# A pooling stage with four bands built and four copied, its scale on the bands, its residual bias on DVE and its order held by the source

## The chip, the cores and the metric

The kernel runs on one core of a Trainium2 chip. The time is the device time of one execution in microseconds, the median of several runs. The core's engines are TensorE (PE in the profile, its weight loads PEld), VectorE (DVE), ScalarE (ACT), GpSimd (POOL) and SyncE (SP), which issues every DMA here. Each engine works through its own queue in order, and semaphores hold one engine back until another has finished what it needs.

## The reference

A trunk of two layers over 512 tokens of 1024 channels, float32 throughout. Layer 0 mixes tokens by causal pooling, layer 1 by windowed attention; each is followed by a gated MLP with a short causal convolution. Only the pooling of layer 0 and the first matmuls of its MLP matter here:

```python
def pool_mixer(h, w, b, scale):          # h: RMS-normed tokens
    csum = jnp.cumsum(hf, axis=1)
    for gi, win in enumerate((2, 4, 8, 16)):      # 256 channels each
        mean = (c - lo) / jnp.minimum(t1, win)    # mean of the last win tokens
        outs.append(mean - hf[..., sl])
    p = jnp.stack(outs, axis=2)
    y = jnp.einsum('bsgc,gcd->bsgd', p, w) + b
    return y.reshape(B, S, D) * scale

h = h + pool_mixer(rms_norm(h, norm_mix[0]), ...)
h = h + conv_glu_ffn(rms_norm(h, norm_ffn[0]), ...)
```

## The kernel before

Channels lie on partitions: the residual h is eight tiles h 0 to h 7 of 128 channels by 512 tokens. Every product of weights and activations is made of three matmuls, since both sides are split into a rounded half (`_h`) and the rest (`_l`): `mm3` (L82) issues h times h at L84, h times l at L85, l times h at L86. ScalarE makes the rounded half, and DVE or POOL subtracts it to get the rest.

The pooling stage (`pool_mixer`, L256) goes like this. POOL first builds eight bands of 128 by 144 (L162 to L172): four for the inner tiles, one for each window, and four for the edge at the first token, where the window is cut and the divisor comes from `rc` (L160). Twelve warm-up products (L263) run on PE meanwhile. For each of four tiles of 128 tokens (L264), ScalarE sums the squares (L266), ScalarE and DVE turn the sum into 1/rms (`rsqrt_mean`, L177), DVE scales the 1024 columns of the token tile by it (L268), and PE multiplies each of the eight channel blocks with its band (L271); a float32 product takes two passes of PE, so a tile has 16. The eight results lie in the eight PSUM banks. Then `split_scaled` (L247) gives px_h on ScalarE (L251) and px_l on DVE (L252) for each bank, with a weight tile of the MLP split behind every second one, its rest on POOL (L99). Last, for each block c: ScalarE adds the bias to h c (L299), PE makes the pooled product (six matmuls), DVE adds it to h c with the scale (L305), `split_scaled` gives f0x_h and f0x_l, and `norm.add` squares h c on ScalarE (L215) and adds it up on POOL (L224). The products use six banks in turn, 0 to 5 and then 0 and 1.

The MLP follows (`mlp_in`): its first group is four products at once in the banks 2 to 5, each over k = 0 to 7, with f0x of block k as the moving side; then the statistics of the norm (L230). A first matmul on a bank waits until the previous content has been read: by L305 of blocks 2 to 5 in this case.

All loads go through SP's queue in the order of the source: four token tiles, two pooling weight tiles, the vectors, three MLP weight tiles, then h 0 to h 7 (L290), and then the weights of the MLP as buffers come free.

The order of each engine's instructions is made by a planner: among the instructions whose inputs its own model of time takes to be ready, the first of the source goes first. So the order on an engine can differ from the source. `tc.keep_in_program_order(ins)` puts `ins` behind the instruction traced just before it on the same engine; nothing in the kernel before uses it.

Of the kernel before, what the change touches and what calls it, by code (L numbers as in the profile page):

```python
# [31 lines left out]
WINDOWS = (2, 4, 8, 16)  # L32
BW = P + 16
# [6 lines left out]
EPS = 1e-6  # L40
# [17 lines left out]
def trunk(ctx: ExitStack, tc: tile.TileContext, x_tok, x_t, vecs, w_pool, w_kq, w_v, w_o, w_in, w_out, out_a, out_b):  # L58
    nc = tc.nc
    V, A, G, T = nc.vector, nc.scalar, nc.gpsimd, nc.tensor  # L60
# [8 lines left out]
    def small(pool, n, words, dt=F32, **kw):  # L69
        return pool.tile([P, words], dt, **kw)[:, :n]  # L70
# [17 lines left out]
    def fetch(src, n, name):  # L88
        raw = wp.tile([P, 1024], F32, tag="raw", name=f"{name}_raw", bufs=3)
        nc.sync.dma_start(raw[:, :n], src)  # L90
        return raw

    def weights(src, n, name, eng=None, raw=None):

        raw = raw or fetch(src, n, name)
        h = wp.tile([P, 1024], F32R, tag="wh", name=f"{name}_h")
        l = wp.tile([P, 1024], F32R, tag="wl", name=f"{name}_l")
        A.activation(h[:, :n], raw[:, :n], AF.Copy)  # L98
        (eng or V).tensor_tensor(l[:, :n], raw[:, :n], h[:, :n].bitcast(F32), ALU.subtract)  # L99
        return h, l  # L100

    def part(w, k, m=P):
        return tuple(t[:, k * m : (k + 1) * m] for t in w)

    def in_weights(layer, j, s, eng=None, raw=None):
        return weights(w_in[layer, j, s], D, f"wi{layer}_{j}_{s}", eng, raw)

    def out_weights(layer, half, m):
        w = [
# [5 lines left out]
    def kept_weights(layer, half, m):  # L115
# [41 lines left out]

    rc = small(fst, 16, 64, name="rc")
    for t in range(15):
        G.memset(rc[:, t : t + 1], 1.0 / (t + 1))  # L160
    band = fst.tile([P, 8, BW], F32, name="band")
    for edge in (True, False):  # L162
        for g, w in enumerate(WINDOWS):
            b = band[:, 4 * edge + g, :]
            G.memset(b, 1.0 / w)
            G.affine_select(b, b, [[1, BW]], ALU.is_ge, 0.0, base=0, channel_multiplier=-1)
            G.affine_select(b, b, [[-1, BW]], ALU.is_ge, 0.0, base=w - 1, channel_multiplier=1)
            G.affine_select(b, b, [[1, BW]], ALU.not_equal, 1.0 / w - 1.0, base=0, channel_multiplier=-1)
            if edge:
                f = b[:, : w - 1]  # L170
                G.affine_select(f, rc[:, : w - 1], [[1, w - 1]], ALU.is_ge, 0.0, base=0, channel_multiplier=-1)
                G.tensor_tensor(f, f, ident[:, : w - 1], ALU.subtract)  # L172
# [4 lines left out]
    def rsqrt_mean(dst, ssq, n, root=False):  # L177


        def tmp(k, dt=F32):  # L180
            return small(sm, n, 16, dt, tag=f"rs_{k}", name=f"rs_{k}", bufs=4)

        v = tmp("v")
        y = tmp("y")
        if root:
            A.activation(y, ssq, AF.Sqrt, bias=eps, scale=1.0 / D)
            V.tensor_scalar(v, ssq, -0.5 / D, -0.5 * EPS, ALU.mult, ALU.add)
            V.reciprocal(y, y)
        else:
            V.tensor_scalar(v, ssq, 1.0 / D, EPS, ALU.mult, ALU.add)  # L190
            sh = tmp("i", I32)
            V.tensor_scalar(sh, v.bitcast(I32), 1, None, ALU.logical_shift_right)
            V.tensor_scalar(y.bitcast(I32), sh, -1.0, float(0x5F3759DF), ALU.mult, ALU.add)
            V.tensor_scalar(v, v, -0.5, None, ALU.mult)
        t = tmp("t")
        steps = 1 if root else 3
        for it in range(steps):
            z = dst if it == steps - 1 else y
            if n == 1:
                V.scalar_tensor_tensor(t, y, y, v, ALU.mult, ALU.mult)  # L200
# [43 lines left out]
            A.activation(rb[:, lo:hi], ps[:, lo:hi], AF.Copy)  # L244
            return rb

    def split_scaled(src, g, name):  # L247

        xh = xp.tile([P, S], F32R, tag="xh", name=f"{name}_h")
        xl = xp.tile([P, S], F32R, tag="xl", name=f"{name}_l")  # L250
        A.activation(xh, src, AF.Copy, scale=g)  # L251
        V.scalar_tensor_tensor(xl, src, g, xh.bitcast(F32), ALU.mult, ALU.subtract)  # L252
        return xh, xl


    def pool_mixer(norm, xs, ws):  # L256
        r0 = small(fst, NT, 32, name="r0")
        ss0 = small(fst, NT, 32, name="ss0")

        warm = small(fst, BW, 192, name="warm")  # L260
        V.memset(warm, 0.0)
        for i in range(12):
            T.matmul(banks[-1][:, :BW], lhsT=warm[:, :P], rhs=warm, start=True, stop=True)  # L263
        for i in range(NT):  # L264
            junk = fst.tile([P, D], F32, tag="junk", name=f"junk{i}")
            A.activation(junk, xt[:, i, :], AF.Square, accum_out=ss0[:, i : i + 1])  # L266
            rsqrt_mean(r0[:, i : i + 1], ss0[:, i : i + 1], 1, root=True)
            V.tensor_scalar(xt[:, i, :], xt[:, i, :], r0[:, i : i + 1], None, ALU.mult)  # L268
            n = min(BW, S - i * P)
            for c in range(NC):  # L270
                T.matmul(  # L271
                    banks[c][:, i * P : i * P + n],
                    lhsT=xt[:, i, c * P : (c + 1) * P],
                    rhs=band[:, (0 if i else 4) + c // 2, :n],
                    start=(i == 0),
                    stop=(i == NT - 1),
                    skip_group_check=True,
                )
        wpool = []
# [11 lines left out]
        pool_x = []
        for c in range(NC):
            pool_x.append(split_scaled(banks[c], col(V_NM + c), f"px{c}"))
            if c % 2:
                ws.append(in_weights(0, *pre[c // 2], G, raws[c // 2]))
# [87 lines left out]
    with tc.tile_pool(name="ap", bufs=2) as ap:  # L383
# [88 lines left out]
        for j in range(NT):  # L472
            ps = vps[j // 2][:, (j % 2) * 256 : (j % 2 + 1) * 256]
# [157 lines left out]
    with tc.tile_pool(name="fp1", bufs=2) as fp:  # L631
# [33 lines left out]
        w = {m: (kept_weights if m == NB else out_weights)(1, 1, m) for m in range(NB, NC)}  # L665
# [5 lines left out]
        for m in range(NB, NC):  # L671
# [15 lines left out]
        ps = bank("aux")  # L687
        for x, t in enumerate((norm3.acc, sq)):
            for j in range(2):
# [3 lines left out]
                    rhs=ones[:, :2],  # L693
# [78 lines left out]
```

## Time and profile before

| | us |
|---|---|
| median of 3 runs (932.06 to 932.5) | 932.32 |
| the profiled execution, its own time | 932.39 |
| its span, first to last instruction | 930.6 |
| PE busy, share of the span | 915.2, 98% |
| DVE busy | 574.8, 62% |
| ACT busy | 427.3, 46% |
| POOL busy | 135.1, 15% |

The busy times are of the whole span. The pooling stage is the first 28 us of it and the first group of the MLP ends at 51 us, so the shares say little about the stage: there one reads the instructions in order of time, with their start, how long they took, and in brackets how long the engine had been idle before and who released it. The ends of matmuls are modelled in the profile; their starts, and the distance from one start to the next, are what counts for PE. A line that stands for several instructions in a row has their number behind an x.

### The profile page before, as it was taken

The page shows a single profiled execution, that of the slowest core. Times are in us where ns is not written, and L with a number is a line of the kernel's source. Part 1 is how long each engine was busy: PE and PEld are TensorE (multiplying, and loading weights), DVE is VectorE, ACT ScalarE, POOL GpSimd, SP SyncE. Part 2 cuts the span into 40 slices and gives each one's busy share as a digit, 9 for nine tenths or more (in the row PEclk, how much of TensorE's full clock was granted, in tenths as well). Part 3 has the DMA queues.
Part 4 walks back from the last instruction along what each step waited for, and adds up shares of the span by engine and source line. Part 5 has one row for each costly group of instructions (what it writes and reads, how often), then busy time and mean ns, then how long its engine had stood idle before and what let it go on. Part 6 is the DMA issues. An engine that isn't in the chain of part 4 may idle for free.

```text
span 930.6 us, 11682 instructions
## 1 busy us (share of the span) xinstructions
PE 915.2 (98%) x4419; PEld 771.5 (83%) x4419; DVE 574.8 (62%) x945; ACT 427.3 (46%) x690; POOL 135.1 (15%) x217
## 2 busy tenths in 40 slices
PE   8999999999999999999899999999999999999996
PEld 7788888888888888898788888888888888888896
DVE  5679766335777754456777482987743377777433
ACT  7655443223444443337787451644422244444532
POOL 9600000000000001325654140000000000000022
PEclk9999999999999999999999999999999999999999
DMA  9133222333223223322111041242233422322312
GB/s 333 67 113 113 93 84 80 93 128 113 91 91 105 65 87 106 114 91 68 50 43 46 2 158 39 98 139 104 63 93 100 136 91 91 111 80 63 95 60 91
DMA packets 28855, 88.13 MB, mean 95 GB/s; under 512 B 3200, under 2 KB 4352, under 8 KB 28800
## 3 DMA queue, kind: packets, MB, share of 16 engines
q1 hardware_dynamic: 28800, 87.40, 28.5%
q8 instruction: 34, 0.56, 0.2%
q14 instruction: 21, 0.17, 0.1%
HBM read 85.29 MB, written 2.10 MB: 94 GB/s over the span
## 4 chain that ended last, share of the span: by engine, by line
PE 92%; ACT 3%; DVE 2%; POOL 2%; issue 1%; POOLq 0%; ACTq 0%
PE bank L84 30%; PE bank L85 30%; PE bank L86 30%; PE bank L548 1%; PE bank L578 1%; ACT sc L565 1%; DVE q L464 1%; ACT px_h L251 0%; POOL sc L570 0%; PE bank L241 0%; ACT q_u L457 0%; DVE sc L551 0%; ACT wi_h L98 0%; PE bank L271 0%; ACT th L581 0%
## 5 line engine op out<-in xcount | busy, mean ns | idle before, releaser
L224 POOL TENSOR_TENSOR n_acc<-n_acc,n_sq 128x512 f32<-128x512 f32 (+1 forms) x28 | 39.1, 1395 | 716.4 <-ACT n_sq L215 709.8
L98 ACT ACTIVATE wi_h<-wi_raw 128x1024 fp32r<-128x1024 f32 x88 | 93.0, 1061 | 109.0 <-PE bank L85 100.5
L85 PE MATMUL bank<-f0x_l,wi_h 128*128 128x512 f32 x352 | 137.1, 389 | 0.8 <-DVE f0x_l L252 0.8
L84 PE MATMUL bank<-f0x_h,wi_h 128*128 128x512 f32 x352 | 137.3, 390 | 0.0
L84 PE MATMUL bank<-f1x_h,wi_h 128*128 128x512 f32 x352 | 137.2, 390 | 0.0
L84 PE MATMUL bank<-zh,wo_h 128*128 128x512 f32 (+1 forms) x363 | 137.1, 378 | 0.0
L86 PE MATMUL bank<-f0x_h,wi_l 128*128 128x512 f32 x352 | 137.0, 389 | 0.0
L86 PE MATMUL bank<-f1x_h,wi_l 128*128 128x512 f32 x352 | 137.0, 389 | 0.0
L85 PE MATMUL bank<-f1x_l,wi_h 128*128 128x512 f32 x352 | 137.0, 389 | 0.0
L86 PE MATMUL bank<-zh,wo_l 128*128 128x512 f32 (+1 forms) x363 | 136.6, 376 | 0.0
L85 PE MATMUL bank<-zl,wo_h 128*128 128x512 f32 (+1 forms) x363 | 136.6, 376 | 0.0
L99 DVE TENSOR_TENSOR wi_l<-wi_raw,wi_h 128x1024 fp32r<-128x1024 f32 x84 | 102.6, 1223 | 49.2 <-ACT wi_h L98 37.3
L98 ACT ACTIVATE wo_h<-wo_raw 128x768 fp32r<-128x768 f32 (+1 forms) x70 | 57.5, 823 | 120.2 <-PE bank L85 108.5
L313 DVE TENSOR_TENSOR c_u<-bank,n_rb 128x512 f32<-128x512 f32 x88 | 59.9, 687 | 75.9 <-PE bank L86 75.9
L99 DVE TENSOR_TENSOR wo_l<-wo_raw,wo_h 128x768 fp32r<-128x768 f32 (+1 forms) x66 | 60.3, 914 | 54.4 <-ACT wo_h L98 54.2
L86 PEld LDWEIGHTS bank<-zh,wo_l 128*128 128x128 f32 x363 | 68.3, 188 | 12.5
L84 PEld LDWEIGHTS bank<-zh,wo_h 128*128 128x128 f32 x363 | 68.3, 188 | 12.3
L85 PEld LDWEIGHTS bank<-zl,wo_h 128*128 128x128 f32 x363 | 68.3, 188 | 12.3
L85 PEld LDWEIGHTS bank<-f0x_l,wi_h 128*128 128x128 f32 x352 | 66.1, 188 | 14.6 <-DVE f0x_l L252 1.2
L84 PEld LDWEIGHTS bank<-f0x_h,wi_h 128*128 128x128 f32 x352 | 66.1, 188 | 14.2 <-DVE h L305 0.4
L86 PEld LDWEIGHTS bank<-f1x_h,wi_l 128*128 128x128 f32 x352 | 66.1, 188 | 13.9
L316 ACT ACTIVATE c_t<-c_u,vec 128x512 f32<-128x512 f32 x88 | 70.6, 811 | 15.3 <-DVE c_u L313 14.5
(173 smaller groups left out, 1488.7 us busy)
## 6 DMA issues: line engine op xcount, KB each, us to landing
wi_raw<-w_in SPq DMA_DIRECT2D x88, 512.0 KB, 3.2
wo_raw<-w_out SPq DMA_DIRECT2D x31, 384.0 KB, 3.0
wo_raw<-w_out SPq DMA_DIRECT2D x31, 320.0 KB, 2.8
kq_raw<-w_kq SPq DMA_DIRECT2D x10, 512.0 KB, 3.2
wo_raw<-w_o SPq DMA_DIRECT2D x8, 512.0 KB, 3.2
xt<-x_tok SPq DMA_DIRECT2D x4, 512.0 KB, 5.2
h<-x_t SPq DMA_DIRECT2D x8, 256.0 KB, 7.5
wpool_raw<-w_pool SPq DMA_DIRECT2D x2, 512.0 KB, 8.5
```

What stands on the lines that cost most here:

```text
L84: T.matmul(ps, lhsT=wh, rhs=xh, start=start, stop=False, **kw)
L85: T.matmul(ps, lhsT=wh, rhs=xl, start=False, stop=False, **kw)
L86: T.matmul(ps, lhsT=wl, rhs=xh, start=False, stop=stop, **kw)
L98: A.activation(h[:, :n], raw[:, :n], AF.Copy)
L99: (eng or V).tensor_tensor(l[:, :n], raw[:, :n], h[:, :n].bitcast(F32), ALU.subtract)
L224: eng.tensor_tensor(self.acc[:, lo:hi], self.acc[:, lo:hi], sq[:, lo:hi], ALU.add)
L313: V.tensor_tensor(u, ps, rb, ALU.mult)
L316: A.activation(t, u, AF.Identity, bias=col(V_CB + layer * 2 * NF + m), scale=cw[2])
L464: V.tensor_tensor(t[dst], u[src], t[src].bitcast(F32), ALU.subtract)
L548: T.matmul(o, lhsT=qt, rhs=kt[:, kk : kk + 256], start=x == 0, stop=x == 1)
L565: A.activation(t, t, AF.Exp, bias=neg[:, i : i + 1], scale=-1.0, accum_out=den[:, i : i + 1])
L578: T.transpose(ps[:, i * P : (i + 1) * P], sc[i // 2][:, i % 2, kb * P : (kb + 1) * P], ident)
```

## The change

Eight parts, all in the pooling stage and in the helpers that it calls:

- POOL builds four bands instead of eight, and the small edge parts apart; the rest of the edge bands is copied by DVE (`edge_copy`), two before the tile loop and two inside the first tile. The memsets of `rc` and of the bands go from POOL to DVE.
- The 1/rms of a token tile scales the four bands (`sband`, 4 x 144 columns) instead of the token tile (1024 columns).
- In the first tile DVE squares and sums half of the columns, ScalarE the other half.
- The rest of the first pooling weight is taken on DVE instead of POOL.
- The rest of an MLP weight tile that POOL makes ahead is made in four instructions of 256 columns instead of one of 1024.
- The bias of h c is added on DVE (`bias`) instead of ScalarE.
- The fourth MLP weight tile is fetched and split behind the last pooled product (step "w").
- `pin` holds the order on DVE and ScalarE. The string `order` gives it: m is the split of a bank (with the MLP weight behind every second one), p the pooled product, b the bias, t the total into h c, n the split of the new h c and its square.

```diff
+    def weights(src, n, name, eng=None, raw=None, step=1024, pin=lambda ins: ins):
...
+        pin(A.activation(h[:, :n], raw[:, :n], AF.Copy))
+        for a in range(0, n, step):
+            o = slice(a, min(a + step, n))
+            (eng or V).tensor_tensor(l[:, o], raw[:, o], h[:, o].bitcast(F32), ALU.subtract)
...
+        return weights(w_in[layer, j, s], D, f"wi{layer}_{j}_{s}", eng, raw, 256 if eng else 1024, pin)
...
+    pin = tc.keep_in_program_order
...
-        G.memset(rc[:, t : t + 1], 1.0 / (t + 1))
+        V.memset(rc[:, t : t + 1], 1.0 / (t + 1))
...
+    def edge_copy(g):
+        a = WINDOWS[g] - 1
+        pin(V.tensor_copy(band[:, 4 + g, a:], band[:, g, a:]))
+    for g, w in enumerate(WINDOWS):
+        b = band[:, g, :]
+        V.memset(b, 1.0 / w)
...
+        f = band[:, 4 + g, : w - 1]
+        G.affine_select(f, rc[:, : w - 1], [[1, w - 1]], ALU.is_ge, 0.0, base=0, channel_multiplier=-1)
+        G.tensor_tensor(f, f, ident[:, : w - 1], ALU.subtract)
+        if g < 2:
+            edge_copy(g)
...
-            V.tensor_scalar(xt[:, i, :], xt[:, i, :], r0[:, i : i + 1], None, ALU.mult)
+            sband = fst.tile([P, 4, BW], F32, tag="sband", name=f"sband{i}", bufs=2)
+            e = 0 if i else 4
+            pin(V.tensor_scalar(sband[:, :, :n], band[:, e : e + 4, :n], r0[:, i : i + 1], None, ALU.mult))
...
-                    rhs=band[:, (0 if i else 4) + c // 2, :n],
+                    rhs=sband[:, c // 2, :n],
...
-            A.activation(h[c], h[c], AF.Identity, bias=bs[:, c : c + 1])
+        def bias(c):
+            pin(V.tensor_scalar(h[c], h[c], bs[:, c : c + 1], None, ALU.add))
+
+        def total(c):
+            pin(V.scalar_tensor_tensor(h[c], ps[c], col(V_PS + c), h[c], ALU.mult, ALU.add))
+
+        def normed(c):
+            xs.append(split_scaled(h[c], col(V_NFF + c), f"f0x{c}", pin))
             norm.add(c)
+        order = "m0 m1 p0 p1 b0 b1 m2 m3 p2 p3 m4 m5 t0 t1 b2 b3 p4 p5 m6 m7 t2 t3 p6 p7 w n0 b4 b5 t4 t5 n1 b6 b7 t6 t7 n2 n3 n4 n5 n6 n7"
+        for step in order.split():
+            if step == "w":
+                ws.append(in_weights(0, *pre[3], G))
...
```

## Rows read from the trace of the kernel before

**Rows 1.** The page, part 1: busy time, share and instructions of each engine.
```profile
PE 915.2 (98%) x4419; PEld 771.5 (83%) x4419; DVE 574.8 (62%) x945; ACT 427.3 (46%) x690; POOL 135.1 (15%) x217
```
**Rows 2.** Waits of PE, whole span: us in total, times, longest us.
```profile
PE bank L85 <- DVE f0x_l L252: 0.8, 1, 0.8
```
**Rows 3.** PE by time, 0 to 52 us: start us, us, what, times, idle before.
```profile
1.17 5.09 PE L263 MATMUL bank<-warm 128*128 128x144 f32 x24 [1.17 <-DVE warm L261]
7.89 0.36 PE L271 MATMUL bank<-band,xt 128*128 128x144 f32 x1 [1.64 <-DVE rs_y L188]
12.52 4.50 PE L271 MATMUL bank<-band,xt 128*128 128x144 f32 x36 [0.35 <-POOL band L168]
17.02 0.50 PE L84 MATMUL bank<-px_h,wpool_h 128*128 128x512 f32 x1
17.82 0.40 PE L84 MATMUL bank<-px_h,wpool_h 128*128 128x512 f32 x1
28.03 0.39 PE L84 MATMUL bank<-f0x_h,wi_h 128*128 128x512 f32 x1
51.13 0.95 PE L230 MATMUL bank<-ones,n_acc 128*128 128x2 f32 x8
```
**Rows 4.** DVE and POOL by time, 24 to 32 us, columns as in rows 3.
```profile
24.88 0.74 DVE L252 SCALAR_TENSOR_TENSOR f0x_l<-h,vec,f0x_h 128x512 fp32r<-128x512 f32 x1
27.80 2.75 DVE L252 SCALAR_TENSOR_TENSOR f0x_l<-h,vec,f0x_h 128x512 fp32r<-128x512 f32 x1 [1.33 <-ACT f0x_h L251]
27.60 2.40 POOL L99 TENSOR_TENSOR wi_l<-wi_raw,wi_h 128x1024 fp32r<-128x1024 f32 x1
29.97 1.73 POOL L224 TENSOR_TENSOR n_acc<-n_acc,n_sq 128x512 f32<-128x512 f32 x1
```
**Rows 5.** DVE and POOL by time, 0 to 12 us, columns as in rows 3.
```profile
0.94 0.56 POOL L160 MEMSET rc<- 128x1 f32 x15
0.94 0.18 DVE L261 MEMSET warm<- 128x144 f32 x1
11.40 0.91 DVE L268 TENSOR_SCALAR xt<-xt,r 128x1024 f32<-128x1024 f32 x1
11.56 0.20 POOL L174 MEMSET ones<- 128x128 f32 x1
```
**Rows 6.** Groups by line, 0 to 60 us: busy us, mean ns, idle before.
```profile
L252 DVE SCALAR_TENSOR_TENSOR px_l<-bank,vec,px_h 128x512 fp32r<-128x512 f32 x8 | 5.5, 744 | 3.7 <-ACT px_h L251 3.7
L305 DVE SCALAR_TENSOR_TENSOR h<-bank,vec,h 128x512 f32<-128x512 f32 x8 | 5.5, 738 | 0.0
L240 DVE TENSOR_SCALAR n_d<-ident,n_r 128x128 f32<-128x128 f32 x4 | 0.9, 281 | 0.1
L285 POOL TENSOR_TENSOR wpool_l<-wpool_raw,wpool_h 128x512 fp32r<-128x512 f32 x4 | 5.0, 1269 | 0.0
L99 POOL TENSOR_TENSOR wi_l<-wi_raw,wi_h 128x1024 fp32r<-128x1024 f32 x4 | 9.6, 2415 | 0.0
```
**Rows 7.** SP: issues of h 0 and h 1, each with its time to landing.
```profile
7.50 0.33 SPq L290 DMA_DIRECT2D h<-x_t  x1
h<-x_t SPq DMA_DIRECT2D x1, 256.0 KB, 9.9
8.73 0.33 SPq L290 DMA_DIRECT2D h<-x_t  x1
h<-x_t SPq DMA_DIRECT2D x1, 256.0 KB, 9.4
```
**Rows 8.** PE after a hole in the attention, and that stretch's busy times (PEclk: granted clock).
```profile
451.64 0.38 PE L548 MATMUL bank<-kh,q 128*128 128x256 f32 x1 [2.86 <-DVE q L464]
454.66 0.63 PE L84 MATMUL bank<-ax_h,kq_h 128*128 128x512 f32 x1
455.09 0.63 PE L85 MATMUL bank<-ax_l,kq_h 128*128 128x512 f32 x1
454.00:456.00 2.00, 2.00 (x9) 1.75 (x8) 2.00 (x10) 1.70 (x10) 0.51 (x2) 0.60 0.00 0
```

More of the change, by code (lines that the diff above doesn't have):

```diff
@@ L91, in fetch @@
         return raw
-    def weights(src, n, name, eng=None, raw=None):
+    def weights(src, n, name, eng=None, raw=None, step=1024, pin=lambda ins: ins):
         raw = raw or fetch(src, n, name)
@@ L97, in weights @@
         l = wp.tile([P, 1024], F32R, tag="wl", name=f"{name}_l")
-        A.activation(h[:, :n], raw[:, :n], AF.Copy)
-        (eng or V).tensor_tensor(l[:, :n], raw[:, :n], h[:, :n].bitcast(F32), ALU.subtract)
+        pin(A.activation(h[:, :n], raw[:, :n], AF.Copy))
+        for a in range(0, n, step):
+            o = slice(a, min(a + step, n))
+            (eng or V).tensor_tensor(l[:, o], raw[:, o], h[:, o].bitcast(F32), ALU.subtract)
         return h, l
@@ L103, in part, with in_weights @@
         return tuple(t[:, k * m : (k + 1) * m] for t in w)
-    def in_weights(layer, j, s, eng=None, raw=None):
-        return weights(w_in[layer, j, s], D, f"wi{layer}_{j}_{s}", eng, raw)
+    def in_weights(layer, j, s, eng=None, raw=None, pin=lambda ins: ins):
+        return weights(w_in[layer, j, s], D, f"wi{layer}_{j}_{s}", eng, raw, 256 if eng else 1024, pin)
     def out_weights(layer, half, m):
@@ L159, in trunk @@
     for t in range(15):
-        G.memset(rc[:, t : t + 1], 1.0 / (t + 1))
+        V.memset(rc[:, t : t + 1], 1.0 / (t + 1))
     band = fst.tile([P, 8, BW], F32, name="band")
[L162 to L172, printed above, removed]
+    def edge_copy(g):
[4 more added lines that the diff above has]
+        V.memset(b, 1.0 / w)
+        G.affine_select(b, b, [[1, BW]], ALU.is_ge, 0.0, base=0, channel_multiplier=-1)
+        G.affine_select(b, b, [[-1, BW]], ALU.is_ge, 0.0, base=w - 1, channel_multiplier=1)
+        G.affine_select(b, b, [[1, BW]], ALU.not_equal, 1.0 / w - 1.0, base=0, channel_multiplier=-1)
+        f = band[:, 4 + g, : w - 1]
[3 more added lines that the diff above has]
+            edge_copy(g)
     ones = cst.tile([P, P], F32, name="ones")
@@ L186, in rsqrt_mean @@
             A.activation(y, ssq, AF.Sqrt, bias=eps, scale=1.0 / D)
-            V.tensor_scalar(v, ssq, -0.5 / D, -0.5 * EPS, ALU.mult, ALU.add)
-            V.reciprocal(y, y)
+            pin(V.tensor_scalar(v, ssq, -0.5 / D, -0.5 * EPS, ALU.mult, ALU.add))
+            pin(V.reciprocal(y, y))
         else:
@@ L245, in spread, with split_scaled @@
             return rb
-    def split_scaled(src, g, name):
+    def split_scaled(src, g, name, pin=lambda ins: ins):
         xh = xp.tile([P, S], F32R, tag="xh", name=f"{name}_h")
         xl = xp.tile([P, S], F32R, tag="xl", name=f"{name}_l")
-        A.activation(xh, src, AF.Copy, scale=g)
-        V.scalar_tensor_tensor(xl, src, g, xh.bitcast(F32), ALU.mult, ALU.subtract)
+        pin(A.activation(xh, src, AF.Copy, scale=g))
+        pin(V.scalar_tensor_tensor(xl, src, g, xh.bitcast(F32), ALU.mult, ALU.subtract))
         return xh, xl
@@ L257, in pool_mixer @@
         r0 = small(fst, NT, 32, name="r0")
-        ss0 = small(fst, NT, 32, name="ss0")
+        ss0 = small(fst, 2 * NT, 32, name="ss0")
         warm = small(fst, BW, 192, name="warm")
@@ L264, in pool_mixer @@
         for i in range(NT):
+            cut = D // 2 if i == 0 else D
             junk = fst.tile([P, D], F32, tag="junk", name=f"junk{i}")
-            A.activation(junk, xt[:, i, :], AF.Square, accum_out=ss0[:, i : i + 1])
+            if cut < D:
+                pin(
+                    V.tensor_tensor_reduce(
+                        out=junk[:, cut:],
+                        in0=xt[:, i, cut:],
+                        in1=xt[:, i, cut:],
+                        scale=1.0,
+                        scalar=0.0,
+                        op0=ALU.mult,
+                        op1=ALU.add,
+                        accum_out=ss0[:, NT : NT + 1],
+                    )
+                )
+            A.activation(junk[:, :cut], xt[:, i, :cut], AF.Square, accum_out=ss0[:, i : i + 1])
+            if cut < D:
+                pin(V.tensor_tensor(ss0[:, i : i + 1], ss0[:, i : i + 1], ss0[:, NT : NT + 1], ALU.add))
+                for g in (2, 3):
+                    edge_copy(g)
             rsqrt_mean(r0[:, i : i + 1], ss0[:, i : i + 1], 1, root=True)
-            V.tensor_scalar(xt[:, i, :], xt[:, i, :], r0[:, i : i + 1], None, ALU.mult)
             n = min(BW, S - i * P)
+            sband = fst.tile([P, 4, BW], F32, tag="sband", name=f"sband{i}", bufs=2)
+            e = 0 if i else 4
+            pin(V.tensor_scalar(sband[:, :, :n], band[:, e : e + 4, :n], r0[:, i : i + 1], None, ALU.mult))
             for c in range(NC):
@@ L284, in pool_mixer, with mixed, product @@
             A.activation(hh, raw, AF.Copy)
-            G.tensor_tensor(ll, raw, hh.bitcast(F32), ALU.subtract)
+            if g:
+                G.tensor_tensor(ll, raw, hh.bitcast(F32), ALU.subtract)
+            else:
+                pin(V.tensor_tensor(ll, raw, hh.bitcast(F32), ALU.subtract))
             wpool.append((hh, ll))
         pre = [(0, 1), (0, 0), (1, 1), (1, 0)]
-        raws = [fetch(w_in[0, j, t], D, f"wi0_{j}_{t}") for j, t in pre[:3]] + [None]
+        raws = [fetch(w_in[0, j, t], D, f"wi0_{j}_{t}") for j, t in pre[:3]]
         for c in range(NC):
             nc.sync.dma_start(h[c], x_t[:, c, :])
[L291 to L295, printed above, removed]
-        bs = small(cst, NC, 64, name="bs")
-        V.tensor_tensor(bs, vec[:, V_PB : V_PB + NC], vec[:, V_PS : V_PS + NC], ALU.mult)
-        for c in range(NC):
-            A.activation(h[c], h[c], AF.Identity, bias=bs[:, c : c + 1])
+        bs = small(cst, NC, 64, name="bs")
+        pin(V.tensor_tensor(bs, vec[:, V_PB : V_PB + NC], vec[:, V_PS : V_PS + NC], ALU.mult))
+        pool_x = {}
+        def mixed(c):
+            pool_x[c] = split_scaled(banks[c], col(V_NM + c), f"px{c}", pin)
+            if c % 2 and c < 7:
+                ws.append(in_weights(0, *pre[c // 2], G, raws[c // 2], pin))
+        def product(c):
             g = c // 2
@@ L304, in pool_mixer @@
                 mm3(ps, w, pool_x[2 * g + k], k == 0, k == 1)
-            V.scalar_tensor_tensor(h[c], ps, col(V_PS + c), h[c], ALU.mult, ALU.add)
-            xs.append(split_scaled(h[c], col(V_NFF + c), f"f0x{c}"))
-            norm.add(c)
+            return ps
+        def bias(c):
[4 more added lines that the diff above has]
+            xs.append(split_scaled(h[c], col(V_NFF + c), f"f0x{c}", pin))
+            norm.add(c)
+        ps = {}
+        order = "m0 m1 p0 p1 b0 b1 m2 m3 p2 p3 m4 m5 t0 t1 b2 b3 p4 p5 m6 m7 t2 t3 p6 p7 w n0 b4 b5 t4 t5 n1 b6 b7 t6 t7 n2 n3 n4 n5 n6 n7"
+        for step in order.split():
+            if step == "w":
+                ws.append(in_weights(0, *pre[3], G))
+                continue
+            c = int(step[1])
+            if step[0] == "p":
+                ps[c] = product(c)
+            else:
+                {"m": mixed, "b": bias, "t": total, "n": normed}[step[0]](c)
     def conv_chunk(fp, layer, ps, rb, m, name):
```

## The prediction, made before the changed kernel ran

> **What bounds the kernel now.** I read the page first: PE is busy 98% of the span [rows 1], so this is a TensorE kernel and only two things move its end: how late PE's continuous stretch begins, and the holes in it afterwards. The waits of PE over the whole run come next: in the first 52 us, the stage that the change touches, the one inside the stretch is 0.8 us for f0x_l [rows 2]. Third, PE in order of time [rows 3]. The warm-up passes take 5.09 us from 1.17; the first band pass starts at 7.89; the last 36 band passes run without a hole from 12.52, just after POOL's last band; the first product (L84 on px_h) starts at 17.02 and the first of f0x at 28.03; the group of four products ends at 51.13, where the eight small statistics matmuls begin. Two starts give the cadence: from 17.82 to 28.03 there are 45 matmuls, (28.03 - 17.82) / 45 = 0.227 us each. A pooled product has 6 of them (1.36 us), the eight products 48 (10.9 us); one k of the first group has 12 (2.72 us), all eight k 96 (21.8 us). What the change is worth is how far it moves the 51.13.
>
> The wait for f0x_l is the key to the rest. DVE's L252 on f0x_l took 2.75 us from 27.80 where its like took 0.74 from 24.88; POOL's L99 was running from 27.60 to 30.00, and POOL's next instruction, n_acc, lasted 1.73 from 29.97 [rows 4]. So DVE stood until POOL's instruction was over (30.00 to 30.55 is 0.55 us of its own work), then POOL stood. An operation with one SBUF input shows it too: the scaling L268 ran from 11.40 to 12.31, the POOL memset that started at 11.56 ended at 11.76, and 12.31 - 11.76 = 0.55 us is left for 1024 columns, the same 0.55 [rows 5]. Operations with a PSUM input don't stand: eight px_l with a mean of 744 ns, eight L305 with 738 [rows 6], while POOL was busy beside most of them. I call the first kind port work and the second free work.
>
> **The change, part by part.**
> **Bands and token scale.** POOL loses four bands, and 15 + 4 memsets go to DVE. They sit ahead of the warm-up's memset. POOL does the 15 in 0.56 us and DVE a memset of 144 columns in 0.18 [rows 5], so they delay the warm-up by 0.56 + 4 x 0.18 = 1.3 us: 1.17 + 1.3 + 5.09 = 7.6, still ahead of 7.89; at 0.18 each they would take 3.4, and the first product would come at 17.7, which DVE's chain below would still cover. The scale moves from 1024 columns of tokens to 576 of bands: 0.28 us for 128 columns [rows 6] and 0.91 for 1024 with the wait in it [rows 5] bound it; about 0.55. The half square on DVE and the copies of two edges go in front of tile 0's scale; they cost between nothing and 0.7 us there (f0x_l's 0.74 is the nearest row for 512 columns with two inputs), against ScalarE's half square saved. I keep 7.89 for the first band pass, give or take 0.7. POOL's bands then end long before PE wants them, so all 64 passes run on at 4.50 / 36 = 0.125 us: 7.89 + 8.0 = 15.9 for the first product, 1.1 us earlier than 17.02.
>
> **The order held by the source.** Each pinned instruction stays behind the one traced before it on its engine, and from px_l 0 on everything on DVE is pinned, so DVE's order is the string's: m0 m1, b0 b1, m2 m3 and so on. Here a wait is added: b0 and b1 read h 0 and h 1, which the queue issues at 7.50 and 8.73 and which land 9.9 and 9.4 us later, at 17.4 and 18.1 [rows 7]. Nothing ahead of them in the queue changes. Behind b1 on DVE stands px_l 2, and behind that p2 (its bank is the one that px_l 2 reads). So DVE goes on from 18.1 whatever the front won: p0 and p1 end at 15.9 + 2.7 = 18.6, px_l 2 at about 19.3, and PE stands 0.7 us.
>
> **Residual bias on DVE.** ScalarE loses eight instructions, which bounds nothing. DVE gains eight port works of 512 columns: half of 0.55 on the port plus the 0.2 that is left of L240's 0.28 for 128 columns [rows 6], so 0.48, or 0.42 from start to start. DVE's chain from h 1's landing to the end of f0x_l 2 now holds 7 biases (2.9), 6 px_l at 0.69 (4.1), 8 L305 at 0.69 (5.5) and 3 f0x_l at 0.70 (2.1): 14.6 us, 18.1 + 14.6 = 32.7. PE's first group can't do without it: its third and fourth banks are those of p4 and p5, freed by t4 and t5, and its third k needs f0x_l 2.
>
> **Port waits in that chain.** POOL has three wpool_l (1269 ns each), four wi_l (2415 each) and seven n_acc (as L285, 1.27) from about 12.5 on, 3.8 + 9.7 + 8.9 = 22.4 us before DVE's own port time stretches it: it is busy through the chain. The change cuts each wi_l into four; at the slope from 1269 for 512 to 2415 for 1024, a quarter takes about 0.67 us [rows 6]. A port work that follows free work meets half a POOL instruction on average, 0.3 or 0.6 us; one that follows another port work lets POOL slip a whole one in, less its own 0.2 of lead: 0.45 beside wi_l, 1.0 beside n_acc. Beside the wi_l I count b1, b2 and f0x_l 0 at 0.25 and b3, b4, b5 at 0.45; beside the n_acc f0x_l 1 at 0.6, b6 and b7 at 1.0, f0x_l 2 at 0.2. That is 0.75 + 1.35 + 2.8 = 4.9 us. From both sides: no wait at all, or a whole POOL instruction for each, 6 x 0.67 + 4 x 1.27 = 9.1. I take 4.9 because the row of f0x_l at 27.80 shows the wait in full.
>
> **Sum.** f0x_l 2 ends at 32.7 + 4.9 = 37.6. From there PE has 11 matmuls of that k and five k: 2.5 + 13.6 = 16.1, so the group ends at 53.7, 2.6 us after 51.13. (It also loses the old hole of 0.8 us, which is inside 51.13.) Nothing behind the group changes. The profiled execution took 932.39 us, 1.8 around its span of 930.6; the median of the runs is 932.32, 0.07 under it. 932.39 + 2.6 = 935.0.
>
> **The rivals.**
> **The biases don't wait.** If the port work of one SBUF input goes on beside POOL's tensor_tensor, the chain keeps its 14.6 us and only the f0x_l wait; PE stands 0.7 for p2 and then runs on: 15.9 + 10.9 + 0.7 + 21.8 = 49.3, 1.8 us under before: 930.6, or 930.0 with a front that is 0.6 faster. For it: all rows of one-input work are beside selects and a memset, none beside a tensor_tensor. Against it: in rows 5 even a memset, which reads nothing, made DVE stand. It decides by the duration of a bias beside L99: at 0.5 us it is this, from about 0.9 the forecast.
> The Trainium skill ("SBUF — State Buffer", section "Who interferes with whom") says that a DVE instruction with at most one SBUF input, outside the two-port modes, doesn't contend with GpSimd, and that tensor_scalar can enter those modes. By the first half the time would be that of this rival; the second half agrees with rows 5, where a tensor_scalar of this kind stood for a memset.
>
> **Half the waits.** If the planner leaves POOL holes, or gives n_acc a later place, the waits come to 2 to 3.5 us and the group to 51 to 52.3: 932 to 933.5.
>
> **The clock falls as well.** PE's holes would be about 0.7 (p2), 1.2 (t4) and 2.2 us (f0x_l 2). Before has a hole of 2.86 us ahead of 451.64; after it the granted clock is 0.60 in 454 to 456 (on the way between 1.2 and 2.4 GHz), and two like matmuls start 0.43 us apart, 454.66 and 455.09, for 0.227 at the full clock [rows 8]. The hole of 1.6 us ahead of 7.89 had no such effect. Some 8 matmuls at 0.2 more are 1.7 us: 936.7, with longer waits up to 938.
>
> **The order isn't what I read.** If something lets px_l 2 pass the biases, the gain of the front stays: 1.1 + 0.8 of the old hole, 930.4.
>
> **How the numbers follow.** Forecast, 933.4 to 936.5: 0.45. Clock: 0.12. Half the waits: 0.18. No wait of the biases: 0.19. Another order: 0.06. The forecast is that of the likeliest, 935.0. Runs of this kernel tell a difference from about 0.2%, 1.9 us: faster is under 930.5, slower over 934.2. Faster: 0.13 of the no-wait case and 0.05 of the last, 0.18. Same: the rest of these two (0.07), all of the half waits (0.18) and 0.05 of the forecast, 0.30. Slower: 0.52. The range for 8 in 10 reaches from 930.3 to 937.6: the ends of 0 and 9.1 us of wait lie at 930.5 and 939.2, and the outer part of the latter is left out.
>
> **What would show it.** In the profile after: the first band pass near 7.9 and the first product near 15.9 (front); a wait of PE for px_l 2 of 0.5 to 1 us ahead of p2, with b0 released by the DMA of h near 17.4 (order); biases of 0.8 to 1.4 us instead of 0.48 where POOL runs, and waits of PE's L84 for L305 (t4) and of L85 for f0x_l (port); f0x_l 2 ending near 37.6 and the statistics near 53.7 (sum). The forecast is wrong if h lands well ahead of 17.4, if biases last 0.5 us throughout, or if PE's waits after 20 us sum to less than 1.

## The result, and the profile after

The median of the changed kernel is 934.61 us (7 executions, 933.59 to 938.26), that of the kernel before beside it 932.31: 2.3 us slower. The ratio, 1.0032 with a 95% interval of [1.0021, 1.0043] (2.0 to 4.0 us), goes by means and is a little higher, since two of the executions took 935.7 and 938.26, with the lowest mean granted clocks (0.995 and 0.993, for 0.996 to 0.998). The prediction was 935.0, in 930.3 to 937.6. The profiled execution took 933.99 us with a span of 932.3, 1.6 more than that of before.

The waits of PE over the whole span of after (us in total, times, longest) answer to [rows 2]:

```profile
PE bank L85 <- DVE f0x_l L259: 2.3, 2, 1.8
...
PE bank L84 <- DVE px_l L259: 1.4, 1, 1.4
PE bank L84 <- DVE h L343: 0.5, 1, 0.5
```

These three are of the pooling stage: 4.2 us in place of 0.8. The longest of the rest, 2.9 us for q, is the attention's, which before has too. PE in order of time in after, 0 to 60 us, only what had idle time before it, and the statistics (start, us, what, times, idle before; compare [rows 3]):

```profile
2.22 5.25 PE L270 MATMUL bank<-warm 128*128 128x144 f32 x24 [2.22 <-DVE warm L268]
7.71 7.93 PE L299 MATMUL bank<-sband,xt 128*128 128x144 f32 x64 [0.25 <-DVE rs_v L194]
17.01 0.50 PE L84 MATMUL bank<-px_h,wpool_h 128*128 128x512 f32 x1 [1.37 <-DVE px_l L259]
30.04 0.50 PE L84 MATMUL bank<-f0x_h,wi_h 128*128 128x512 f32 x1 [0.48 <-DVE h L343]
32.44 0.50 PE L85 MATMUL bank<-f0x_l,wi_h 128*128 128x512 f32 x1 [0.52 <-DVE f0x_l L259]
37.28 0.50 PE L85 MATMUL bank<-f0x_l,wi_h 128*128 128x512 f32 x1 [1.83 <-DVE f0x_l L259]
53.52 0.95 PE L237 MATMUL bank<-ones,n_acc 128*128 128x2 f32 x8
```

Read it downwards. All 64 band passes run in one piece and end at 15.64, where the pieces of before ended at 17.02. Then PE stands 1.37 us, and the first product starts at 17.01, within 0.01 us of before: the front's gain is gone at once. There is no hole ahead of p2. Three holes follow, which grow from 0.48 to 1.83, and the statistics start at 53.52, 2.39 later than before. By the attention's start the two kernels are still 2.38 apart (454.02 for 451.64); some microseconds later, after the stretch in which both have the clock lowered, 2.0 are left, and 1.7 at the end of the span.

DVE in order of time in after, 11 to 43 us (same columns), the lines that carry the chain:

```profile
11.94 1.52 DVE L297 TENSOR_SCALAR sband<-band,r 128x512 f32<-128x512 f32 x1 [0.51 <-PE bank L299]
13.38 1.75 DVE L316 TENSOR_TENSOR wpool_l<-wpool_raw,wpool_h 128x512 fp32r<-128x512 f32 x1
15.06 1.24 DVE L323 TENSOR_TENSOR bs<-vec 128x8 f32<-128x8 f32 x1
16.22 1.40 DVE L259 SCALAR_TENSOR_TENSOR px_l<-bank,vec,px_h 128x512 fp32r<-128x512 f32 x2
17.54 1.46 DVE L340 TENSOR_SCALAR h<-h,bs 128x512 f32<-128x512 f32 x2
...
27.48 1.84 DVE L340 TENSOR_SCALAR h<-h,bs 128x512 f32<-128x512 f32 x2
29.25 1.40 DVE L343 SCALAR_TENSOR_TENSOR h<-bank,vec,h 128x512 f32<-128x512 f32 x2
30.57 1.82 DVE L259 SCALAR_TENSOR_TENSOR f0x_l<-h,vec,f0x_h 128x512 fp32r<-128x512 f32 x1
32.31 2.94 DVE L340 TENSOR_SCALAR h<-h,bs 128x512 f32<-128x512 f32 x2
35.18 1.40 DVE L343 SCALAR_TENSOR_TENSOR h<-bank,vec,h 128x512 f32<-128x512 f32 x2
36.50 6.13 DVE L259 SCALAR_TENSOR_TENSOR f0x_l<-h,vec,f0x_h 128x512 fp32r<-128x512 f32 x6
```

and POOL in the same stretch:

```profile
11.90 4.37 POOL L314 TENSOR_TENSOR wpool_l<-wpool_raw,wpool_h 128x512 fp32r<-128x512 f32 x3 [5.26 <-ACT wpool_h L312]
16.41 12.64 POOL L101 TENSOR_TENSOR wi_l<-wi_raw,wi_h 128x256 fp32r<-128x256 f32 x16
29.00 7.38 POOL L231 TENSOR_TENSOR n_acc<-n_acc,n_sq 128x512 f32<-128x512 f32 x5
```

DVE is never idle from 12 to 42 us, so each of its waits is inside an instruction: nothing shows as idle time, and the wait has to be read from the duration. L343 and px_l, which read a PSUM bank, last 1.40 a pair throughout. Those that work on SBUF alone stretch where they have to wait for an instruction of POOL: a bias lasts 0.51 us where it meets only the end of one (b2, from 22.87; POOL's quarter of wi_l ends at 23.10), 0.96 right behind other work of this kind, beside a whole quarter (L101, mean 826 ns), and 1.51 beside n_acc. They don't all wait: f0x_l 0, at 26.82, took 0.73 with POOL busy. The biases stand in two lines, the instructions on tile h from 22 to 24 us and from 32 to 34 us (shortest, median, longest in ns):

```profile
L340 DVE TENSOR_SCALAR h<-h,bs x2: 512/736/959, 22.9 to 23.3; 128x512 f32<-128x512 f32 x2
L340 DVE TENSOR_SCALAR h<-h,bs x2: 1511/1511/1511, 32.3 to 33.7; 128x512 f32<-128x512 f32 x2
```

### The profile page after: what moved, and what is told of

It is laid out like the page before. It is cut to its first block, busy times and chain, and to the rows that moved or that the text cites. A ratio compares the mean times of both kernels' runs of the same rounds, so it can differ in the third digit from the quotient of the medians.

```text
span 932.3 us, 11687 instructions
## 1 busy us (share of the span) xinstructions
PE 914.9 (98%) x4419; PEld 771.6 (83%) x4419; DVE 584.9 (63%) x980; ACT 422.0 (45%) x682; POOL 131.2 (14%) x193
## 4 chain that ended last, share of the span: by engine, by line
PE 90%; DVE 5%; ACT 3%; issue 1%; POOL 0%; DMA 0%; DVEq 0%; ACTq 0%; POOLq 0%
PE bank L84 29%; PE bank L86 29%; PE bank L85 29%; PE bank L601 1%; ACT sc L618 1%; DVE q L517 1%; PE bank L631 1%; DVE tl L635 1%; ACT q_u L510 1%; ACT q L516 0%; DVE h L340 0%; DVE h L343 0%; PE bank L299 0%; ACT th L634 0%; DVE px_l L259 0%
## 5 line engine op out<-in xcount | busy, mean ns | idle before, releaser
L101 DVE TENSOR_TENSOR wi_l<-wi_raw,wi_h 128x1024 fp32r<-128x1024 f32 x84 | 102.7, 1225 | 49.0 <-ACT wi_h L98 46.7
L101 DVE TENSOR_TENSOR wo_l<-wo_raw,wo_h 128x768 fp32r<-128x768 f32 (+1 forms) x66 | 60.4, 915 | 54.5 <-ACT wo_h L98 54.3
L86 PEld LDWEIGHTS bank<-f0x_h,wi_l 128*128 128x128 f32 x352 | 66.1, 188 | 13.8
```

The source lines that it names most:

```text
L86: T.matmul(ps, lhsT=wl, rhs=xh, start=False, stop=stop, **kw)
L101: (eng or V).tensor_tensor(l[:, o], raw[:, o], h[:, o].bitcast(F32), ALU.subtract)
```

## The experiments

Two theories stood against each other. Mine: DVE's chain sets the end of the stage, made longer by the biases and by their waits for the port that POOL holds; the front's gain is lost on DVE as well. The rivals: the end is set by the landing of h, by the order of the steps, or by the clock. In each case the ratio is to the kernel before, on the same chip. Two changed kernels are compared by their medians, and their difference is resolved only where their intervals don't overlap.

**Bias back on ScalarE.**

```diff
-            pin(V.tensor_scalar(h[c], h[c], bs[:, c : c + 1], None, ALU.add))
+            pin(A.activation(h[c], h[c], AF.Identity, bias=bs[:, c : c + 1]))
```

> One part undone: the eight biases go back to ScalarE, pinned at the same places of the same string. If DVE's chain and its waits for POOL cost the time, the 7.7 us that the eight biases take on DVE in the changed kernel (1.47 + 1.47 + 1.84 + 2.94) leave the chain, f0x_l 2 ends near 30 instead of 37.2 and PE runs on after its first product at 17.0: 17.0 + 10.9 + 21.8 = 49.7 and a hole of 0.2 to 0.5 ahead of p2 (px_h 2 now waits behind the bias of h 1, which lands at 17.9), so the statistics begin near 50 instead of 53.5 and the time is 931.0 to 931.5, 3.2 under the changed kernel. If the loss came from elsewhere (the front, the clock), PE keeps its holes of 0.5, 0.5 and 1.8 us and the time stays at 934.6. If ScalarE becomes the bound with eight more instructions of 0.7 us, PE waits for f0x_h and the time is 933 to 934.

Measured: 932.1 us, 1.0005 [0.9996, 1.0014]. With everything else of the change in place, the loss is gone: it belongs to the bias on DVE. The other seven parts together bring nothing that these runs resolve. PE and ScalarE by time, then DVE and POOL at the front:

```profile
15.92 0.50 PE L84 MATMUL bank<-px_h,wpool_h 128*128 128x512 f32 x1 [0.33 <-DVE px_l L259]
21.07 0.50 PE L84 MATMUL bank<-px_h,wpool_h 128*128 128x512 f32 x1 [2.09 <-DVE px_l L259]
51.17 0.95 PE L237 MATMUL bank<-ones,n_acc 128*128 128x2 f32 x8
```
```profile
17.67 0.72 ACT L340 ACTIVATE h<-h,bs 128x512 f32<-128x512 f32 x1 [1.40 <-DMA h<-x_t]
18.93 0.72 ACT L340 ACTIVATE h<-h,bs 128x512 f32<-128x512 f32 x1 [0.53 <-DMA h<-x_t]
19.56 1.25 ACT L258 ACTIVATE px_h<-bank,vec 128x512 fp32r<-128x512 f32 x2
```
```profile
11.88 0.49 DVE L297 TENSOR_SCALAR sband<-band,r 128x512 f32<-128x512 f32 x1 [0.35 <-PE bank L299]
12.11 4.32 POOL L314 TENSOR_TENSOR wpool_l<-wpool_raw,wpool_h 128x512 fp32r<-128x512 f32 x3 [5.52 <-ACT wpool_h L312]
```

Here the first product starts at 15.92, as predicted for the change itself. Nothing in the edit does that: the fourth scaled band starts 0.23 us ahead of POOL's first wpool_l and takes 0.49, where in after it starts 0.04 behind and takes 1.52. The time is half a microsecond above the expected 931.0 to 931.5, which goes with one hole of 2.09: ScalarE waits for h 0 and h 1, and px_h 2 stands behind that. After it PE runs on without a hole. So the hole that I had predicted on DVE is real as soon as the front is early.

**No additions of squares on POOL.** The sums of squares are left out.

```diff
-            norm.add(c)
+            norm.add(c) if c == 0 else norm.square(c, 0, S)
```

> The seven additions of squares on POOL (n_acc) are left out in the pooling stage; the squares stay. Nothing else moves. If the waits for POOL's port are the cost, f0x_l 1 falls from 1.82 to 0.75 us, the biases of h 6 and h 7 from 1.51 each to 0.5, f0x_l 2 ends near 34.1 instead of 37.2, PE's hole of 1.8 us goes, and the group ends at 50.5 to 51: 931.6 to 932.1. If DVE's own work is the cost and the waits lie beside something else, it stays within 0.3 of the changed kernel, 934.3 to 934.9.

Measured: 931.4 us, 0.9991 [0.9982, 0.9999], just under the expected 931.6 to 932.1. DVE by time, 30 to 38 us:

```profile
30.49 0.73 DVE L259 SCALAR_TENSOR_TENSOR f0x_l<-h,vec,f0x_h 128x512 fp32r<-128x512 f32 x1
31.15 0.87 DVE L340 TENSOR_SCALAR h<-h,bs 128x512 f32<-128x512 f32 x2
31.94 1.40 DVE L343 SCALAR_TENSOR_TENSOR h<-bank,vec,h 128x512 f32<-128x512 f32 x2
33.26 4.05 DVE L259 SCALAR_TENSOR_TENSOR f0x_l<-h,vec,f0x_h 128x512 fp32r<-128x512 f32 x6
```

The same instructions, with POOL still: f0x_l 1 goes from 1.82 to 0.73, b6 and b7 from 2.94 to 0.87, and f0x_l 2 starts 3.24 us earlier. The holes at 32.44 and 37.28 are gone and the statistics start at 50.54. Three DVE instructions beside n_acc are thus worth the whole loss.

**Whole wi_l on POOL instead of quarters.**

```diff
-        return weights(w_in[layer, j, s], D, f"wi{layer}_{j}_{s}", eng, raw, 256 if eng else 1024, pin)
+        return weights(w_in[layer, j, s], D, f"wi{layer}_{j}_{s}", eng, raw, 1024, pin)
```

> One part undone: POOL makes the rest of each MLP weight tile in one instruction of 1024 columns (2.4 us) instead of four of 256. If a port work waits for the whole POOL instruction in flight, the second bias of each pair and f0x_l 0 wait up to 2.3 us instead of 0.45: 3 to 6 us more in DVE's chain and a time of 937 to 940. If DVE gets the port in shares, it stays or gains a little (POOL saves 3 us of its own): 934.0 to 934.6.

Measured: 936.99 us, 1.0049 [1.0036, 1.0061], at the lower end of the expected 937 to 940. One DVE line and what it did to PE:

```profile
17.65 4.01 DVE L340 TENSOR_SCALAR h<-h,bs 128x512 f32<-128x512 f32 x2 [1.03 <-DMA h<-x_t]
```
```profile
22.37 0.80 PE L84 MATMUL bank<-px_h,wpool_h 128*128 128x512 f32 x1 [3.35 <-DVE px_l L259]
```

The length of POOL's instruction sets the price: b0 and b1 take 4.01 us beside wi_l of about 2.4 us each and 1.46 beside the quarters. The hole of 3.35 also holds DVE's wait of 1.03 for h, since here too the front was early (first product at 16.01). Behind it the granted clock is 0.50 from 22 to 26 us, but DVE's chain is later still, with holes of 0.33 and 0.48 at 35.11 and 40.23, and sets the end. By the medians the quarters are worth 936.99 - 934.61 = 2.4 us to the change; the intervals overlap. In the two profiled executions the statistics are 2.98 us apart (56.50 for 53.52).

**Bias on DVE in the kernel before, and nothing else.**

```diff
-            A.activation(h[c], h[c], AF.Identity, bias=bs[:, c : c + 1])
+            V.tensor_scalar(h[c], h[c], bs[:, c : c + 1], None, ALU.add)
```

> The kernel before with one part alone: its eight biases on DVE instead of ScalarE, everything else as it was, the planner's order included. If a bias on DVE costs by POOL's port, the biases stand behind wi_l instructions of 2.4 us each and behind n_acc, 0.5 to 2.5 us each instead of 0.5, and f0x_l comes later by 4 us or more: 934 to 938. If the bias is nearly free on DVE and the loss of the changed kernel comes from its held order, the time stays at 932.3.

Measured: 938.72 us, 1.0064 [1.0051, 1.0078], above the expected 934 to 938. DVE, POOL and PE by time:

```profile
29.09 3.63 DVE L299 TENSOR_SCALAR h<-h,bs 128x512 f32<-128x512 f32 x2
```
```profile
28.64 2.40 POOL L99 TENSOR_TENSOR wi_l<-wi_raw,wi_h 128x1024 fp32r<-128x1024 f32 x1 [3.85 <-ACT wi_h L98]
31.00 4.51 POOL L224 TENSOR_TENSOR n_acc<-n_acc,n_sq 128x512 f32<-128x512 f32 x3
```
```profile
35.11 0.79 PE L84 MATMUL bank<-f0x_h,wi_h 128*128 128x512 f32 x1 [4.00 <-DVE h L305]
```

Without the quarters and the held order the bias alone costs 6.5 us by the medians; the change as a whole, 2.3, loses about 4 less. Not all of the 6.5 is waiting for POOL. Behind the hole of 4.00 the granted clock is 0.50 from 34 to 40 us: the 12 matmuls from 35.11 to 40.39 take 5.28 us, for 2.7 at the cadence of before, so up to 2.6 us are the clock's, in the profiled execution (939.6).

**The front put right.** Four buffers for the scaled bands instead of two, the first wpool_l back on POOL, and the small product bs just ahead of b0.

```diff
-            sband = fst.tile([P, 4, BW], F32, tag="sband", name=f"sband{i}", bufs=2)
+            sband = fst.tile([P, 4, BW], F32, tag="sband", name=f"sband{i}", bufs=4)
...
-            if g:
-                G.tensor_tensor(ll, raw, hh.bitcast(F32), ALU.subtract)
-            else:
-                pin(V.tensor_tensor(ll, raw, hh.bitcast(F32), ALU.subtract))
+            G.tensor_tensor(ll, raw, hh.bitcast(F32), ALU.subtract)
```

> The three things ahead of px_l 0 on DVE are taken out of its way: four buffers for the scaled bands instead of two, the rest of the first pooling weight on POOL, and the small product of bias and scale ahead of the first bias instead of ahead of px_l 0. px_l 0 should then start near 14.8 instead of 16.2 and the first product near 15.6 instead of 17.0. If the landing of h 0 and h 1 (17.2 and 17.9) sets DVE's chain next, as the prediction has it, the gain is lost ahead of p2: PE's hole of 1.4 us moves from before the first product to before p2, b1 still ends near 18.7, and the time is 934.0 to 934.6. If the front sets the end, 1.4 us are gained: 933.2.

Measured: 934.87 us, 1.0034 [1.0025, 1.0043]; no gain, as expected, and slightly above the range. DVE and PE by time:

```profile
15.02 1.41 DVE L259 SCALAR_TENSOR_TENSOR px_l<-bank,vec,px_h 128x512 fp32r<-128x512 f32 x2 [1.84 <-ACT px_h L258]
18.00 1.36 DVE L338 TENSOR_SCALAR h<-h,bs 128x512 f32<-128x512 f32 x2 [1.20 <-DMA h<-x_t]
```
```profile
15.82 0.50 PE L84 MATMUL bank<-px_h,wpool_h 128*128 128x512 f32 x1
20.08 0.50 PE L84 MATMUL bank<-px_h,wpool_h 128*128 128x512 f32 x1 [1.24 <-DVE px_l L259]
...
37.62 0.50 PE L85 MATMUL bank<-f0x_l,wi_h 128*128 128x512 f32 x1 [1.81 <-DVE f0x_l L259]
```

px_l 0 starts 1.2 us earlier and the first product at 15.82, as I had predicted for the change. Then DVE waits 1.20 us for h, and PE gives all of it back in a hole of 1.24 ahead of p2. The chain behind starts 0.36 us later than in after (px_l 2 at 19.28 for 18.92), and its last hole is the same.

**No held order.**

```diff
-    pin = tc.keep_in_program_order
+    pin = lambda ins: ins
```

> The changed kernel with nothing held: every instruction that was held behind its forerunner is left to the planner. In the built program DVE then has b0 and b1 ahead of px_l 0, px_l 1, and ScalarE has three MLP weight halves ahead of px_h 0. If a held-up DVE chain sets the end (my theory): DVE stands for h 0 and h 1 (landing 17.2 and 17.9 in the changed kernel) with two px_l still to come, so the chain that began at 18.04 there carries 1.4 us more, PE's first product with px_l comes near 19 instead of 17.2, the statistics near 55 instead of 53.5, and the time is 935.5 to 937.5. Rival: the order held by the source gives nothing, the planner's order is worth the same since the port waits only move elsewhere: 934 to 935.

Measured: 936.38 us, 1.0047 [1.0032, 1.0061], in the expected range, though only partly by the expected way. PE by time:

```profile
11.04 9.60 PE L299 MATMUL bank<-sband,xt 128*128 128x144 f32 x64 [2.70 <-DVE sband L297]
...
39.91 0.50 PE L85 MATMUL bank<-f0x_l,wi_h 128*128 128x512 f32 x1 [1.82 <-DVE f0x_l L259]
56.16 0.95 PE L237 MATMUL bank<-ones,n_acc 128*128 128x2 f32 x8
```

The bands start 3.3 us later, since the planner puts the copies and the scale of the first tile behind the 1/rms of others. b0 therefore starts at 17.89 without a wait for h, and it is the late front, not b0, that holds px_l 0 until 19.84. The last hole of 1.82 is as in after. By the medians the held order is worth about 1.8 us to the change, mainly at the front; the intervals overlap, so that size is not resolved. In the two profiled executions the statistics are 2.64 us apart. What the order of the late steps alone is worth, this run doesn't separate.

**Two splits pulled forward.** n2 and n3 ahead of b6, b7, t6 and t7.

```diff
-... n1 b6 b7 t6 t7 n2 n3 n4 n5 n6 n7
+... n1 n2 n3 b6 b7 t6 t7 n4 n5 n6 n7
```

> Only the string is changed: n2 and n3 stand ahead of b6 b7 t6 t7 instead of behind. PE's first group needs f0x_l 2 for its third k, but t6 and t7 only for its seventh and eighth. If the chain ahead of f0x_l 2 is the cost, it loses two biases (2.94 us with their waits) and two totals (1.3): f0x_l 2 ends near 33.7 instead of 37.2, PE's hole of 1.8 us goes, and at most 0.5 comes back ahead of f0x_l 4, which now stands behind the four. Statistics at 51.6 to 52.1, time 932.4 to 932.9. If DVE's sum and not its order is the limit, the hole moves whole to f0x_l 4 and the time stays at 934.6.

Measured: 933.14 us, 1.0009 [1.0, 1.0018]. That is 1.5 us better than the change, and its profiled execution has no hole of over 0.5 us behind the first product, with the statistics at 51.40. The waits themselves stay (f0x_l 1 to 3 take 5.21 us in a row beside n_acc); they stand where PE still has work in store. The expected 932.4 to 932.9 was somewhat too low.

**The additions moved behind the splits and onto DVE.**

```diff
-            norm.add(c)
...
+        norm.add(0)
+        for c in range(1, NC):
+            sq = norm.square(c, 0, S)
+            pin(V.tensor_tensor(norm.acc, norm.acc, sq, ALU.add))
```

> The seven additions of squares leave POOL and follow on DVE behind f0x_l 7; the computation is whole. If n_acc on POOL costs only by its port, this does what leaving them out did: f0x_l 2 ends near 34, f0x_l 7 near 37.5, the seven additions take 0.7 us each and end near 43, eight us ahead of the statistics at 50.5; time 931.2 to 931.8. If DVE has no room for 5 us more, the statistics wait for it and the time is 933 or more.

Measured: 931.5 us, 0.9991 [0.9982, 1.0], the same as with the additions left out. On DVE they take 5.39 us from 37.59 on, behind f0x_l 7, where nobody waits for DVE.

**All together.** The front put right, the additions behind, n2 and n3 forward, and b0, b1 behind p2, p3.

```diff
-... p0 p1 b0 b1 m2 m3 p2 p3 m4 m5 t0 t1 b2 b3 p4 p5 m6 m7 t2 t3 p6 p7 w n0 b4 b5 t4 t5 n1 b6 b7 t6 t7 n2 n3 n4 ...
+... p0 p1 m2 m3 p2 p3 b0 b1 m4 m5 t0 t1 b2 b3 p4 p5 m6 m7 t2 t3 p6 p7 w n0 b4 b5 t4 t5 n1 n2 n3 b6 b7 t6 t7 n4 ...
```

> The front freed (four scaled bands, the first pooling weight's rest on POOL, the small product behind px_l 3), b0 and b1 behind m2 m3, n2 and n3 ahead of b6 b7, and the additions last on DVE. Each removes one of the waits found so far: first product near 15.7, no wait for h's landing ahead of px_l 2, no hole for f0x_l 2. PE then runs 15.7 + 10.9 + 21.8 = 48.4 with holes of at most 1.2 us in all (t4 behind two biases): statistics at 48.6 to 49.6, against 51.1 before the change, and a time of 929.5 to 931.0, under both kernels. If a bound that I haven't seen stands at 50 to 51 (ScalarE, the weights' landing), it is 931.5 to 932.5.

Measured: 931.05 us, 0.9986 [0.9977, 0.9995]: 1.2 us under the kernel before and 3.6 under the change, at the upper end of the expected 929.5 to 931.0. PE by time:

```profile
15.59 0.50 PE L84 MATMUL bank<-px_h,wpool_h 128*128 128x512 f32 x1
24.99 0.50 PE L85 MATMUL bank<-px_l,wpool_h 128*128 128x512 f32 x1 [0.62 <-DVE px_l L259]
30.05 0.50 PE L84 MATMUL bank<-f0x_h,wi_h 128*128 128x512 f32 x1 [0.45 <-DVE h L341]
50.14 0.95 PE L237 MATMUL bank<-ones,n_acc 128*128 128x2 f32 x8
```

The front's gain now survives, since b0's wait for h has px_l 2 and px_l 3 ahead of it. The statistics, at 50.14, missed the expected 48.6 to 49.6. From 15.59 to there are 144 matmuls, 32.7 us at the cadence, so 1.9 us are lost on the way, where 1.2 were allowed. It is the best of the kernels here; its lead over the one with the additions moved alone (931.5) is not resolved. Nor is it shown that the bias on DVE helps it: the same kernel with the bias on ScalarE was not run.

## Why the prediction came out right, and where it did not

**The front: mis-sized by 1.1 us.** The first band pass was to start at 7.89 (7.71) and all passes to run on (they did, to 15.64). The failed step is "15.9 for the first product". I let that product follow the last pass, and did not follow its bank: it overwrites bank 0, which px_l 0 reads, and ahead of px_l 0 on DVE now stand three port works: the fourth scaled band, which also had to wait for one of two buffers, wpool_l 0 and bs. In after they take 1.52, 1.75 and 1.24 us beside POOL's wpool_l. I had put the scale at 0.55 and had not charged it or the two others with a wait, though my own rule said that they would have one. The experiment on the front shows it: with those out of the way the product starts at 15.82. It takes little to tip: with the same front the fourth band took 0.49, and the product started at 15.92 and 16.01, with the bias on ScalarE and with whole wi_l, where POOL's first wpool_l began 0.23 and 0.36 us behind that band instead of 0.04 ahead of it. So 15.9 was within reach of this front, and the profiled execution of after fell on the other side.

**The hole ahead of p2: mis-sized by 0.7.** It was to follow from an early front and a late h. With the front late there was nothing to wait for: b0 started at 17.54 with h 0 already there. The mechanism was right (holes of 1.24 and 2.09 where the front was put right and where the bias was on ScalarE). Both misses meet at one point: b1 started at 18.04, and I had the chain start at 18.1, for another reason. That is luck in the step, and why the sum still held.

**The chain: right in sum.** From 18.04 to the end of f0x_l 2 at 37.23 are 19.2 us; I had 14.6 of work and 4.9 of waits, 19.5. Of starts to next starts: an instruction with PSUM takes 0.66 (I had 0.69), a pair of biases without POOL 0.79 (31.15 to 31.94 with the additions left out). The work is then 6 px_l, 8 totals and 3 f0x_l at 0.66 and 7 biases at 0.395, 14.0. The waits are what each pair has above 0.79: 0.5 for b1, 0.5, 1.0 and 2.1 for the other pairs, and 1.1 for f0x_l 1, together 5.2. I had b6 and b7 at 1.0 each and b3, b4, b5 at 0.45 each, and these held. The others did not one by one: b2, f0x_l 0 and f0x_l 2 had no wait, where I counted 0.25, 0.25 and 0.2, while b1 had 0.25 and f0x_l 1 0.5 more than I counted. That these cancel is luck.

**The end of the group: right.** 16.1 us from f0x_l 2 to the statistics were predicted, 16.24 measured (37.28 to 53.52), so 53.5 for the predicted 53.7. "Nothing behind the group changes" was short: of the 2.39 us at the statistics, 1.6 reached the profiled execution's time; the median, 2.3 above that of before, kept nearly all of it.

**The rivals.** That the biases don't wait is refuted by their durations, 0.51 to 1.51 us in one kernel, and by two whole kernels: with the additions left out b6 and b7 fall from 2.94 us to 0.87, and with POOL's instructions longer b0 and b1 rise from 1.46 to 4.01. The Trainium skill ("SBUF — State Buffer", section "Who interferes with whom") names tensor_scalar among the operations that can take both ports; the trace agrees with that half of the rule, for a float32 tensor_scalar of 512 columns. Half the waits is refuted by the sum of 5.2. The order was what the string says. The clock did not fall in the stage in the profiled execution of after, though it has holes of 0.48 and 1.83 us where the prediction had 1.2 and 2.2 (t4 and f0x_l 2). It did in the kernel with the front put right, behind a hole of the same length (busy times by stretch; PEclk, the granted clock, is the third number from the end):

```profile
38.00:40.00 2.00, 2.00 (x7) 1.52 (x6) 2.00 (x3) 0.72 (x2) 1.92 (x2) 0.64 0.00 0
40.00:42.00 2.00, 2.00 (x6) 1.60 (x5) 2.00 (x2) 0.00 (x0) 1.06 (x1) 0.51 0.00 0
```

and in after:

```profile
38.00:40.00 2.00, 2.00 (x11) 1.63 (x10) 2.00 (x2) 0.39 (x1) 1.92 (x2) 1.00 0.00 0
```

PE starts 7 and 6 matmuls in 2 us instead of 11, near 1.2 for 2.4 GHz, and there the statistics start at 55.45, 1.93 us later than in after. At the end of the program only 0.8 of it is left (934.78 for 933.99), and the attention shows why. Behind its hole of 2.9 us the granted clock falls in before (0.55 and 0.60 in the two stretches from 452 us) and in after (0.50 and 0.76 from 454), but stays at 1.00 behind the same hole in the kernel with the front put right and in the one with nothing held. So one execution of such a kernel can lose some 2 us in the stage and get about 1 back later; how often each happens, the profiles don't show.

## What to carry to other kernels

An operation that is moved to DVE and works on SBUF alone cost, in these kernels, its own time plus up to the rest of whatever POOL was doing, so price it by the length of POOL's instructions beside it: 0.4 us of work became up to 0.9 beside quarters, 1.4 beside n_acc and 2 in the mean beside whole wi_l. Where such a move is wanted, first get POOL out of the stretch (here the additions, which could wait) or cut its instructions, and only then move. And for each predicted start of a matmul follow its bank to the last reader, and that reader's queue, before a gain is booked.

## What was not expected of the hardware

- The wait leaves no idle time. In after DVE is never idle from 12 to 42 us while it loses over 5 us; only durations of like instructions show it (bias 0.51, 0.96, 1.51), as they did in [rows 4].
- The size of a port work hardly matters beside POOL: bs, with 8 columns, took 1.24 us in after, where POOL ran its wpool_l. With nothing held, a one-column step of the 1/rms (L211) took 1.23 there instead of its usual 0.16, and bs, right behind it, slipped through in 0.15.
- POOL's instructions are stretched too. The prediction priced n_acc by wpool_l's 1.27 us [rows 6]; n_acc itself has a mean of 1478 ns in after, and had 1563 already in before. A quarter of wi_l has 826 ns (the shortest 0.73) for the 0.67 that I had estimated.
- A hole of 1.81 us was followed by a granted clock near 0.5 in one kernel, and holes of 1.82, 1.83 and 2.09 in three others by 1.00; in the attention holes of 2.84 to 2.88 were followed by either. The length of a hole alone did not decide it here. Behind the two longest of the pooling stage, 3.35 (whole wi_l) and 4.00 (bias alone), it was 0.50.
